# One hybrid layer on one core: larger mixer transfers, a lighter second gate-up group, another order in the second down run

## The chip, the core and the metric

The kernel computes one encoder layer on one NeuronCore of a Trainium2 chip. TensorE (PE; its weight loads are PEld) multiplies matrices, VectorE (DVE) and ScalarE (ACT) do elementwise work, GpSimd (POOL) does a little, and SyncE (SP) issues nearly all transfers from device memory. The metric is the device time of one execution in microseconds. The median of three runs of the kernel before is 1865.89 us (1864.14 to 1866.34).

## The reference, cut to what matters

```
x: (1, 256, 2048) float32, all weights float32; D_FF = 5632
x = x + 0.5 * post1(swiglu_1(pre1(x)))            # gate_up 2048 x 11264, down 5632 x 2048
h = pre_m(x);  p = h @ w_mix_in                   # 2048 x 6656
   p -> q, i, f_fwd, f_bwd, g (1024 columns each) | attention q (1024), k, v (256 each)
y_h = bidirectional gated linear recurrence per head, normalised, times silu(g)
y_a = attention within +-128 positions, with a sink logit and a relative bias
x = x + post_m(concat(y_h, y_a) @ w_mix_out)      # 2048 x 2048
x = x + 0.5 * post2(swiglu_2(pre2(x)))
```

With 256 rows of x, every weight is used once per execution and has to come from device memory.

## The kernel before, in words

**Products.** To keep float32 accuracy each operand is split into a high part h and a low part l, and each product is made of three matmuls: h with h, l with h, h with l. The split of a weight tile of 128x1024 is a cast on ACT (L186) followed by a subtraction on DVE (L187). A weight block arrives as 1 MB in a tile `raw` (three of them, and a part of the tile `rooms` as a fourth while the FFN runs), in two transfers of 512 KB issued by SP (L162), and is split in two halves into tiles h and l, of which there are five each.

**Plain and seven.** FFN and output projections work on blocks u of 256 rows of the weight by 1024 columns, for two row blocks m and two column blocks n. A plain block takes eight products (24 matmuls of 512 columns, `plain`). A seven (`seven`, L455 on) forms sums of the weight's quarters on DVE (L466, L470, L472) and of the activations, and needs seven products (21 matmuls); four of the seven go to PSUM banks of their own and are folded into the results at the end of the run (`fold`, L509 to L517). Its last split half can only be cast when L472 is done. `self.sums` holds the blocks for which sums of activations exist. A down or output run that follows a seven with a plain block loads the plain block and splits its first half inside the seven (`AHEAD`).

**One FFN.** The gate and up projections run in 11 column groups of 512 (`Gated`, eight blocks u each, L938 on in `ffn`). In group 0 the activations are not yet scaled by the row statistics, and no sums exist. While it runs, `even(u)` multiplies each block's activations by a power of two (L877) and, for blocks 1, 3 and 5 (`MIXED_IN`), forms their sums (L883, L390 to L394, then a split). All eight calls of `even` are made during blocks 4 to 7 of group 0. Groups 1 to 10 have three sevens each. After each group `units` applies silu (L900) and the product (L901), transposes (L912) and splits the result into `ht` (L920 and L187). The down projection (`Pairs`) makes two runs over 22 blocks, each run for one half of the 2048 columns, with 11 sevens per run (the even blocks up to 16, and 20 and 21); a list per run in `orders` gives the order. The end of the second run (`finish`) is written out by hand, together with the first products of the stage that follows.

**The mixer.** `w_mix_in` is loaded in 52 blocks of 1 MB, by `source_N` (3-D source, 4 or 8 row tiles) and `chunk_T` (8 row tiles), all through `load` (L149). Products of four head pairs are interleaved with the recurrence and the attention of earlier heads (`side_step`): softmax (L1394), transposes of the probabilities (L1409), their copy to SBUF on ACT (L1412, tile `pt`) and their product with v (L1420). The recurrence needs a logarithm (L1222) and several exponentials (L1240, L1242, L1250, L1257), the gates need a sigmoid (L1327, L1444, L1445); a change of function family on ACT comes with an `ACT_TABLE_LOAD`.

**What sets the order.** Outside the stretches under `manual_schedule` a scheduler of the framework orders each engine's instructions from its own estimates of when operands are ready; on the chip each engine then executes its list in order, and waits on semaphores. So an edit at one place can reorder instructions at others.

Of the kernel before, what the change touches and what calls it, by code (L numbers as in the profile page):

```python
# [24 lines left out]
KT = D // P  # L25
# [12 lines left out]
def hymba_layer_kernel(  # L38
# [41 lines left out]
    def pa():  # L80
        return psum.tile([P, 512], F32, tag="pa", name=nm("pa"))

    def pb():
        return psum.tile([P, 512], F32, tag="pb", name=nm("pb"))
# [59 lines left out]
    def new_raw():  # L144

        raw_places.append(raw_places.pop(0))
        return raw_places[-1]

    def load(src, between=None):  # L149
        raw = new_raw()  # L150
        if len(src.shape) == 4:

            dst = raw.rearrange("p (a n b) -> p a n b", a=src.shape[1], n=src.shape[2])
            parts = [(dst[:, a], src[:, a]) for a in range(src.shape[1])]
        else:
            n = src.shape[1]
            dst = raw.rearrange("p (a b) -> p a b", a=n)
            parts = [(dst[:, a : a + n // 2], src[:, a : a + n // 2]) for a in (0, n // 2)]
        for i, (to, of) in enumerate(parts):
            if i and between:  # L160
                between()
            nc.sync.dma_start(to, of)  # L162
        return raw

    def split_load(src, hp=hip, lp=lop, between=None, middle=None):
        return split(load(src, between), hp, lp, middle)
# [230 lines left out]
    class Blocks:  # L397
# [7 lines left out]
        def __init__(self, tiles, sums):  # L405
            self.tiles, self.sums = tiles, sums

        def begin(self, order, c=None):

            self.order, self.pos, self.seen = order, 0, {}  # L410
            self.c = c or [[pa(), pa()], [pb(), pb()]]
            self.p = None
            at = [i for i, u in enumerate(order) if u in self.sums]
            some = len(at)
            plain = len(order) - some
            self.after = at[-1] + 1 if at else len(order) - 1

            self.rest = 6 * (len(order) - self.after - 1)
            self.of = {}
            for i in range(4):  # L420
                self.of["p", i] = 3 * some
                self.of["c", i // 2, i % 2] = 6 * plain + (3 * some if i < 3 else 0)
# [103 lines left out]
        def work(self, upto):  # L526

            while self.pos < upto:
                u = self.order[self.pos]
                if u in self.sums:  # L530
                    v = self.order[self.pos + 1]
                    if self.AHEAD and v not in self.sums and self.pos + 1 < upto:
                        self.ahead = [v]
                        self.seven(u, self.begin_next)
                    else:
                        self.seven(u)
                else:
                    if self.ahead:
                        _, raw, h, l = self.ahead
                        self.ahead = None  # L540
                        hs, ls = zip((h, l), split_half(raw, 1))
                    else:
                        hs, ls = split_load(self.source(u))
                    if self.pos == self.after + 1:
                        self.fold()
                    places = [(k, m, n) for k in range(2) for m in range(2) for n in range(2)]
                    if self.pos in (self.after, self.after + 1):

                        places.sort(key=lambda at: at[1:])
                    for k, m, n in places:  # L550
                        self.plain(u, hs, ls, m, n, k)
                self.pos += 1
# [251 lines left out]
    MIXED_IN = (1, 3, 5)  # L804
# [5 lines left out]
    class Gated(Blocks):  # L810
# [6 lines left out]

        def group(self, g, c=None):
            self.g = g
            self.begin([0, 2, 1, 4, 3, 5, 6, 7] if g == 1 else range(KT // 2), c)  # L820

        def source(self, u):
            return self.w[:, 2 * u : 2 * u + 2, :, self.g * 512 : (self.g + 1) * 512]
# [30 lines left out]
    def ffn(gated, w_dn, post_gain, again, gain=None, lead=None, aside=None):  # L854

        with ExitStack() as st:
# [78 lines left out]
            for g in range(NG):  # L935
                if g:
                    gated.group(g)
                for u in range(gated.pos, KT // 2):  # L938
                    gated.work(u + 1)
                    if g == 0:  # L940
                        if u == 4:
                            power_and_rest()
                            spread(two)
                        for done in {4: (0, 1, 2), 5: (3, 4), 6: (5, 6), 7: (7,)}.get(u, ()):
                            even(done)
                        if u == 5 and aside:
                            aside()
                        if u == 6:
                            raw_places.append(where_X_was(2))
                    if waiting and u == 0:  # L950
                        next(waiting)
                waiting = units(gated.c, rest if g else rs2)
                next(waiting)
# [1 line left out]
            orders = [  # L955
                [1, 3, 0, 5, 2, 7, 4, 9, 6, 11, 8, 10, 13, 12, 15, 14, 16, 17, 20, 21, 18, 19],

                [1, 0, 2, 3, 4, 5, 6, 14, 7, 8, 9, 10, 16, 11, 12, 13, 20, 21, 15, 17, 18, 19],
            ]
            sums.update((u, None) for u in MIXED if u not in sums)  # L960
            rows = Pairs(w_dn, orders, hts, sums, work, post_gain, stored=True)
# [126 lines left out]
    def again_from(src):  # L1088
# [6 lines left out]

    vbanks = [pa(), pa()]
    xt = ffn(
        gated,
        w_ffn1_down[0],
# [451 lines left out]
```

## Time and profile before

| | |
|---|---|
| median of three runs (range) | 1865.89 us (1864.14 to 1866.34) |
| the profiled execution: time, span | 1864.14 us, 1862.4 us |
| PE busy, share of the span | 1833.9 us, 98% |
| DVE busy | 1646.6 us, 88% |
| ACT busy | 1111.1 us, 60% |
| mean granted TensorE clock | 0.998 |

The profile is of one execution. A wait that the views print is the idle time of an engine ahead of an instruction, with the instruction that ended it. Matmuls overlap, so a row of one matmul is longer than the distance to the next one. In the order, names carry the program's buffer numbers; the profile leaves them out.

### The profile page before, as it was taken

Reading aid. Unit: us, or ns where it says so; the run is one execution under the profiler, and the core shown is the slowest. Engines: PE = TensorE matmul, PEld = TensorE weight load, DVE = VectorE, ACT = ScalarE, POOL = GpSimd, SP = SyncE. Lnnn points to the kernel's source line nnn. Section 1 sums busy time; section 2 is a strip of 40 time slices with the busy share of each in tenths; the row PEclk is TensorE's granted clock in tenths of the full one; section 3 lists DMA queues with packets and bytes.
Section 4 is the critical chain, followed back from the end, with each engine's and each line's share of the span. In section 5 each row is a group of like instructions: output and inputs, shape, how many; then the busy total and the mean of one; then the engine's idle time right before and its main releaser. Section 6 shows DMA issues by size and latency. Waiting matters only on the chain.

```text
span 1862.4 us, 24094 instructions
## 1 busy us (share of the span) xinstructions
PE 1833.9 (98%) x8598; PEld 1518.4 (82%) x8598; DVE 1646.6 (88%) x2080; ACT 1111.1 (60%) x1477; POOL 32.7 (2%) x61
## 2 busy tenths in 40 slices
PE   9999999999999999999999999999999999999998
PEld 7788888888888787888888887778888888888786
DVE  7999999999999997577777887999999999899996
ACT  6555556555655555577677655656556555555563
POOL 1000000000000000000000000000000000000000
PEclk9999999999999999999999999999999999999999
DMA  8566656666877775665564565666666665687774
GB/s 285 167 226 228 204 193 206 221 205 204 288 264 261 259 249 203 194 185 152 161 182 138 181 204 180 219 209 211 222 205 214 221 214 200 228 285 258 246 271 160
DMA packets 192889, 400.45 MB, mean 215 GB/s; under 512 B 12809, under 2 KB 60001, under 8 KB 192001
## 3 DMA queue, kind: packets, MB, share of 16 engines
q1 hardware_dynamic: 189248, 387.25, 63.0%
q0 software_dynamic: 3520, 11.67, 1.6%
q8 instruction: 67, 1.10, 0.2%
q14 instruction: 54, 0.43, 0.1%
HBM read 383.12 MB, written 15.75 MB: 214 GB/s over the span
## 4 chain that ended last, share of the span: by engine, by line
PE 71%; DVE 15%; issue 5%; ACT 4%; DMA 4%; POOL 0%; SPq 0%; DVEq 0%; ACTq 0%; POOLq 0%
PE pa L433 29%; PE pb L433 27%; DVE l L187 7%; PE pa L309 6%; PE pa L314 3%; ACT h L186 2%; DMA raw<-in_w_ffn_down_dram 1%; DMA bias<-row 1%; PE pa L364 1%; PE pa L362 1%; PE pa L363 1%; DVE raw L470 1%; DVE raw L472 1%; DVE raw L466 1%; DMA rooms<-in_w_ffn_down_dram 1%
## 5 line engine op out<-in xcount | busy, mean ns | idle before, releaser
L186 ACT CAST h<-raw 128x1024 fp32r<-128x1024 f32 (+1 forms) x691 | 681.1, 1014 | 455.5 <-DVE raw L472 139.4
L187 DVE TENSOR_TENSOR l<-raw,h 128x1024 fp32r<-128x1024 f32 (+1 forms) x691 | 795.7, 1175 | 96.4 <-ACT h L186 57.7
L433 PE MATMUL pa<-h,xt 128*128 128x512 f32 x1168 | 407.2, 393 | 0.4 <-ACT h L186 0.2
L433 PE MATMUL pb<-h,xt 128*128 128x512 f32 x1048 | 366.0, 391 | 0.0
L433 PEld LDWEIGHTS pa<-h,xt 128*128 128x128 f32 x1168 | 219.5, 188 | 46.5 <-ACT h L186 2.1
L433 PEld LDWEIGHTS pb<-h,xt 128*128 128x128 f32 x1048 | 197.0, 188 | 40.9 <-ACT h L186 0.2
L433 PE MATMUL pa<-l,xt 128*128 128x512 f32 x584 | 227.9, 391 | 0.0
L433 PE MATMUL pb<-l,xt 128*128 128x512 f32 x524 | 204.4, 390 | 0.0
L186 ACT CAST h<-rooms 128x1024 fp32r<-128x1024 f32 (+1 forms) x142 | 145.9, 1044 | 69.6 <-DVE rooms L472 39.2
L187 DVE TENSOR_TENSOR l<-rooms,h 128x1024 fp32r<-128x1024 f32 (+1 forms) x142 | 170.0, 1213 | 14.2 <-ACT h L186 14.0
L309 PE MATMUL pa<-xt,h 128*128 128x512 f32 x672 | 165.4, 395 | 0.0
L433 PE MATMUL pa<-h,ht 128*128 128x512 f32 x440 | 156.5, 392 | 1.5 <-DVE pa L511 1.1
L433 PE MATMUL pb<-h,ht 128*128 128x512 f32 x440 | 155.1, 391 | 0.4 <-DVE pb L515 0.4
L309 PEld LDWEIGHTS pa<-xt,h 128*128 128x128 f32 x672 | 123.5, 189 | 23.5
L433 PEld LDWEIGHTS pa<-l,xt 128*128 128x128 f32 x584 | 110.0, 188 | 22.7 <-DVE l L187 0.5
L433 PEld LDWEIGHTS pb<-l,xt 128*128 128x128 f32 x524 | 98.5, 188 | 20.4
L466 DVE TENSOR_TENSOR raw<-raw 128x1024 f32<-128x1024 f32 x92 | 112.4, 1222 | 0.6
L433 PEld LDWEIGHTS pa<-h,ht 128*128 128x128 f32 x440 | 82.7, 188 | 20.5 <-DVE pa L514 1.8
L433 PEld LDWEIGHTS pb<-h,ht 128*128 128x128 f32 x440 | 82.7, 188 | 18.3 <-DVE pb L515 1.3
L314 PE MATMUL pa<-xt,l 128*128 128x256 f32 x672 | 92.6, 288 | 0.0
L433 PE MATMUL pb<-h,xs 128*128 128x512 f32 x240 | 88.4, 397 | 2.5 <-ACT h L186 2.1
L314 PEld LDWEIGHTS pa<-xt,l 128*128 128x128 f32 x672 | 88.1, 193 | 3.3
(278 smaller groups left out, 2505.9 us busy)
## 6 DMA issues: line engine op xcount, KB each, us to landing
raw<-in_w_ffn_gate_up_dram SPq DMA_DIRECT2D x270, 512.0 KB, 4.9
raw<-in_w_ffn_down_dram SPq DMA_DIRECT2D x132, 512.0 KB, 5.2
raw<-in_w_mix_in_dram SPq DMA_DIRECT2D x104, 512.0 KB, 4.3
rooms<-in_w_ffn_gate_up_dram SPq DMA_DIRECT2D x80, 512.0 KB, 5.3
rooms<-in_w_ffn_down_dram SPq DMA_DIRECT2D x44, 512.0 KB, 5.0
sp<-ss SPq DMA_DIRECT2D x44, 512.0 KB, 6.5
raw<-in_w_mix_out_dram SPq DMA_DIRECT2D x32, 512.0 KB, 4.7
ss<-rooms POOLq DMA_DIRECT2D x22, 512.0 KB, 2.9
```

Source lines behind the costliest of these rows:

```text
L186: nc.scalar.copy(hi, src)
L187: nc.vector.tensor_tensor(lo, src, hi.bitcast(F32), ALU.subtract)
L309: nc.tensor.matmul(slot[f], weights(hs, kk, f), xcol(xt, k), start=(k == 0), stop=(k == KT - 1))
L314: nc.tensor.matmul(slot[f][:, 0:T], weights(ls, kk, f), xcol(xt, kh * 8 + kk, 0), start=False, stop=False,)
L362: nc.tensor.matmul(dst, xh, h[:, o : o + n], start=(k == 0), stop=False)
L363: nc.tensor.matmul(dst, xh, l[:, o : o + n], start=False, stop=False)
L364: nc.tensor.matmul(dst, xl, h[:, o : o + n], start=False, stop=(k == KT - 1))
L433: nc.tensor.matmul(self.bank(at), lhs, rhs, start=(n == 1), stop=n in (ends, self.of[at]), skip_group_check=n > ends,)
L466: nc.vector.tensor_tensor(four[:, 0:2], four[:, 0::3], four[:, 1:2].to_broadcast([P, 2, 512]), ALU.add)
L470: nc.vector.tensor_tensor(b22, b11, b22, ALU.add)
L472: nc.vector.tensor_tensor(b21, b22, b21, ALU.add)
```

## The change

Three edits. First, `load` brings a 3-D source in one transfer unless it has exactly two row tiles; these, the blocks of the down and output projections, still come in two. So the 52 blocks of `w_mix_in` come in one transfer of 1 MB each; gate-up blocks have a 4-D source and are as before. Second, group 1 of each gate-up takes its blocks in natural order and has sevens for blocks 3 and 5 only (`begin` gets a list `some`; block 1 becomes plain), and `even(6)` and `even(7)` are called within group 1, after its blocks 1 and 2. Third, the second down run has another order, in which blocks 2 and 3 change places and blocks 14 and 16 stand later.

```diff
@@ load
             n = src.shape[1]
             dst = raw.rearrange("p (a b) -> p a b", a=n)
-            parts = [(dst[:, a : a + n // 2], src[:, a : a + n // 2]) for a in (0, n // 2)]
+            parts = [(dst, src)]
+            if n == 2:
+                parts = [(dst[:, a], src[:, a]) for a in range(2)]
@@ Blocks.begin
-        def begin(self, order, c=None):
+        def begin(self, order, c=None, some=None):
+            self.some = {u for u in some or order if u in self.sums}
...
-            at = [i for i, u in enumerate(order) if u in self.sums]
+            at = [i for i, u in enumerate(order) if u in self.some]
@@ Blocks.work
-                if u in self.sums:
+                if u in self.some:
                     v = self.order[self.pos + 1]
-                    if self.AHEAD and v not in self.sums and self.pos + 1 < upto:
+                    if self.AHEAD and v not in self.some and self.pos + 1 < upto:
@@ Gated.group
-            self.begin([0, 2, 1, 4, 3, 5, 6, 7] if g == 1 else range(KT // 2), c)
+            self.begin(range(KT // 2), c, MIXED_IN[1:] if g == 1 else MIXED_IN)
@@ ffn
                     gated.work(u + 1)
+                    if g == 1 and 1 <= u <= 2:
+                        even(u + 5)
...
-                        for done in {4: (0, 1, 2), 5: (3, 4), 6: (5, 6), 7: (7,)}.get(u, ()):
+                        for done in {4: (0, 1, 2), 5: (3, 4), 6: (5,)}.get(u, ()):
...
-                [1, 0, 2, 3, 4, 5, 6, 14, 7, 8, 9, 10, 16, 11, 12, 13, 20, 21, 15, 17, 18, 19],
+                [1, 0, 3, 2, 4, 5, 6, 7, 8, 14, 9, 10, 11, 12, 16, 13, 20, 21, 15, 17, 18, 19],
```

The added lines shift the numbers: a line of the old file is called by a number higher by 2 to 5 in the new one.

DVE at the start of group 1 of the first FFN, before: the products of group 0's units (`L901`), the splits `l`, the sums of the first seven's weights (`L466`, `L470`, block 1 in `rooms`), and the results' split `ht`.

```order
L901 SCALAR_TENSOR_TENSOR rooms_473<-pa_120,scales,rooms_473 128x512
L187 TENSOR_TENSOR l_727<-rooms_473,h_726 128x512
L901 SCALAR_TENSOR_TENSOR rooms_473<-pb_122,scales,rooms_473 128x512
L466 TENSOR_TENSOR rooms_473<-rooms_473 128x1024
L187 TENSOR_TENSOR l_732<-rooms_473,h_731 128x1024
L390 TENSOR_TENSOR rooms_473<-rooms_473 128x256
L470 TENSOR_TENSOR rooms_473<-rooms_473 128x512
L187 TENSOR_TENSOR ht_677<-rooms_473,ht_677 128x2x256
L393 TENSOR_TENSOR rooms_473<-rooms_473 128x128
L187 TENSOR_TENSOR ht_687<-pb_667,ht_687 128x2x256
L394 TENSOR_TENSOR rooms_473<-rooms_473 128x128
L187 TENSOR_TENSOR l_737<-rooms_473,h_736 128x1024
```

The same place now: `rooms` holds plain block 2, the first seven is block 3 in `raw_114`, and the scaling of block 7 (`L880`, before `L877`) stands here.

```order
L904 SCALAR_TENSOR_TENSOR rooms_473<-pa_120,scales,rooms_473 128x512
L189 TENSOR_TENSOR l_730<-rooms_473,h_729 128x1024
L904 SCALAR_TENSOR_TENSOR rooms_473<-pb_122,scales,rooms_473 128x512
L880 TENSOR_TENSOR xt_127<-xt_127,R 128x1024
L189 TENSOR_TENSOR l_761<-raw_114,h_760 128x512
L392 TENSOR_TENSOR rooms_473<-rooms_473 128x256
L469 TENSOR_TENSOR raw_114<-raw_114 128x1024
L189 TENSOR_TENSOR ht_675<-rooms_473,ht_675 128x2x256
L395 TENSOR_TENSOR rooms_473<-rooms_473 128x128
L189 TENSOR_TENSOR ht_685<-pb_665,ht_685 128x2x256
L396 TENSOR_TENSOR rooms_473<-rooms_473 128x128
L189 TENSOR_TENSOR l_766<-raw_114,h_765 128x1024
```

The first seven is now the fourth block of the group instead of the third, and one scaling has moved in ahead of its weight sums.

ACT in the mixer before, ahead of the copies `pt` of the first attention heads (`kx`, `qd` and `sg` are the recurrence's exponentials and the gate's sigmoid, `yh` the cast of the gated result):

```order
L1250 ACT_TABLE_LOAD
L1250 ACTIVATE kx_7478<-cum_7468 128x128 x2
L186 CAST h_7379<-raw_114 128x1024
L1327 ACT_TABLE_LOAD
L1327 ACTIVATE sg_7242<-g_7236 128x512
L186 CAST h_7417<-raw_112 128x1024
L1240 ACT_TABLE_LOAD
L1240 ACTIVATE qd_7472<-dm_7470 128x512
L186 CAST yh_7247<-ot_6973 128x2x256
L1412 COPY pt_7290<-pb_7291 128x4x128
L1412 COPY pt_7290<-pb_7297 128x4x128
```

And now:

```order
L1245 ACTIVATE qd_7436<-dm_7434 128x512
L1247 ACTIVATE kd_7438<-dm_7434 128x512
L796 COPY g_7204<-pa_7101 128x256
L796 COPY g_7204<-pa_7102 128x256
L188 CAST h_7340<-raw_114 128x1024
L1255 ACTIVATE kx_7442<-cum_7432 128x128 x2
L188 CAST h_7344<-raw_114 128x1024
L1262 ACTIVATE qx_7443<-cum_7432 128x256
L188 CAST h_7381<-raw_112 128x1024
L1332 ACT_TABLE_LOAD
L1332 ACTIVATE sg_7210<-g_7204 128x512
L1417 COPY pt_7257<-pb_7258 128x4x128
```

The logarithm and its table load (`L1227`, before `L1222`) now stand ahead of the softmax, so that all exponentials follow each other: of three table loads ahead of `pt` in this piece one is left, `yh` has moved behind `pt`, and `kd` and `qx` have moved ahead of it. PE's order in the mixer is the same as before.

DVE in the second down run of the first FFN, before: `la` begins a seven, `L466`, `L470` and `L472` are its weight sums. `raw_114` is block 0, `raw_112` block 2, `raw_113` the plain block 3.

```order
L187 TENSOR_TENSOR la_5052<-raw_112,ha_5051 128x512
L466 TENSOR_TENSOR raw_112<-raw_112 128x1024
L187 TENSOR_TENSOR l_5017<-raw_114,h_5016 128x1024
L187 TENSOR_TENSOR l_5057<-raw_112,h_5056 128x1024
L187 TENSOR_TENSOR l_5062<-raw_112,h_5061 128x1024
L470 TENSOR_TENSOR raw_112<-raw_112 128x512
L187 TENSOR_TENSOR l_5067<-raw_113,h_5066 128x1024
L472 TENSOR_TENSOR raw_112<-raw_112 128x512
```

And now, with `raw_112` the plain block 3, `raw_113` block 2 and `rooms` block 4:

```order
L189 TENSOR_TENSOR la_5076<-raw_113,ha_5075 128x512
L189 TENSOR_TENSOR l_5015<-raw_114,h_5014 128x1024
L189 TENSOR_TENSOR l_5044<-raw_112,h_5043 128x1024
L469 TENSOR_TENSOR raw_113<-raw_113 128x1024
L189 TENSOR_TENSOR l_5081<-raw_113,h_5080 128x1024
L189 TENSOR_TENSOR la_5122<-rooms_473,ha_5121 128x512
L473 TENSOR_TENSOR raw_113<-raw_113 128x512
L189 TENSOR_TENSOR l_5086<-raw_113,h_5085 128x1024
L475 TENSOR_TENSOR raw_113<-raw_113 128x512
```

The second half of the plain block 3 and the first operations of block 4 now stand among those of block 2. On the whole PE has six matmuls more, ACT eight table loads fewer, and SP 52 mixer transfers fewer.

## The prediction, made before the run

> **What bounds the kernel now.** I read the page first (busy time, then the chain of work that ended last), then what PE waits for, then PE by stretches.
>
> ```profile
> span 1862.4 us, 24094 instructions
> PE 1833.9 (98%) x8598; PEld 1518.4 (82%) x8598; DVE 1646.6 (88%) x2080; ACT 1111.1 (60%) x1477; POOL 32.7 (2%) x61
> PE 71%; DVE 15%; issue 5%; ACT 4%; DMA 4%; POOL 0%; SPq 0%; DVEq 0%; ACTq 0%; POOLq 0%
> ...
> PE pb L1420 <- ACT pt L1412: 4.9, 3, 1.9
> PE pb L433 <- ACT h L186: 4.0, 5, 1.1
> ```
>
> PE is the bound, and the chain runs mostly through it. The last two rows, of PE's waits (us in total, times, longest), are where it starves longest: a copy on ACT in the mixer, and the cast of a weight half. Both are touched by the change. So it can win only what PE waits there, and loses each matmul that it adds. The stretches show how much (us, then busy time and instructions of each engine; the last two numbers are the transfer engines' share and GB/s):
>
> ```profile
> 60.00:104.00 44.00, 42.10 (x185) 33.42 (x185) 42.45 (x52) 24.15 (x30) 0.59 (x1) 1.00 0.66 216
> 163.00:206.00 43.00, 43.00 (x195) 35.46 (x194) 40.99 (x48) 25.65 (x30) 0.53 (x1) 1.00 0.62 209
> 1200.00:1244.00 44.00, 42.70 (x188) 33.69 (x187) 42.51 (x54) 26.52 (x32) 0.60 (x1) 1.00 0.61 203
> ...
> 163.25 2.72 PE pa L433 x12
> ```
>
> The second row is a later group without waits: 195 PE instructions in 43.00 us, 0.2205 each. Group 1 of the first FFN lies in the first row: 185 instructions would need 40.8 us and took 44.00, so 3.2 us are lost. For the second FFN: 188 x 0.2205 = 41.45, so 2.55 lost. The last row, of the chain, gives the price of one matmul of 512 columns: 2.72 / 12 = 0.227 us.
>
> **Group 1: two sevens in place of three.** The longest wait of group 1 is that of its first seven for the last cast:
>
> ```profile
> 74.40 0.50 PE L433 MATMUL pb<-h,xs 128*128 128x512 f32 x1 [1.08 <-ACT h L186]
> ...
> 72.59 0.69 DVE L472 TENSOR_TENSOR rooms<-rooms 128x512 f32<-128x512 f32 x1
> 690.85 5.76 DVE L187 TENSOR_TENSOR l<-raw,h 128x1024 fp32r<-128x1024 f32 x5
> ```
>
> ACT is idle ahead of that cast; DVE is late with L472. DVE's prices, start to start: an operation of 1024 columns about 1.14 (last row: 5.76 / 5 with the tail of the fifth), one of 512 about 0.60 (run 2's rows below: 612.17 to 612.77). A seven has four of the first and three of the second: 6.4 us on DVE against 21 x 0.227 = 4.76 on PE. A plain block has two: 2.3 against 24 x 0.227 = 5.44. So a seven costs the lead 1.65 us, a plain block restores 3.1. A group has slack on average, but group 1 starts with DVE behind: `even`, the sums and group 0's results come in the same 25 us.
>
> Now one plain block more stands ahead of the first seven: PE asks 5.44 us later. DVE's added work up to that point, by the order, is two splits of that plain block, 2.3 us; in the second FFN the moved L880 stands ahead too, but it stood ahead of the old first seven as well. The new margin is 5.44 - 2.3 - 1.25 (the wait, with the distance to the next matmul) = about 1.9 us; the second seven has a plain block before it and keeps about 2. So the waits go. `even(6)` and `even(7)` cost 1.14 each as before and are needed only by blocks 6 and 7, over 20 us later; without that cover a late one would cost PE up to 1.14. I take back 5.2 of the 5.75 us (bounds: 3.0, if the interleaved remainder stays, and 5.75). **The price:** block 1 as a plain block has three matmuls more, in two FFNs six: 6 x 0.227 = +1.36 us, all on PE.
>
> **Second down run.** Blocks 0 and 2 are two sevens in a row, right after DVE's work on the first run's results:
>
> ```profile
> 612.17 0.68 DVE L470 TENSOR_TENSOR raw<-raw 128x512 f32<-128x512 f32 x1
> 612.77 1.22 DVE L187 TENSOR_TENSOR l<-raw,h 128x1024 fp32r<-128x1024 f32 x1
> 613.90 0.69 DVE L472 TENSOR_TENSOR raw<-raw 128x512 f32<-128x512 f32 x1
> 614.70 2.00 ACT L186 CAST h<-raw 128x1024 fp32r<-128x1024 f32 x2 [3.24 <-DVE raw L472]
> 615.80 0.50 PE L433 MATMUL pb<-h,sp 128*128 128x512 f32 x1 [0.93 <-ACT h L186]
> ...
> 1753.63 0.50 PE L433 MATMUL pb<-h,sp 128*128 128x512 f32 x1 [0.93 <-ACT h L186]
> 683.43 1.23 DVE L187 TENSOR_TENSOR l<-rooms,h 128x1024 fp32r<-128x1024 f32 x1 [1.19 <-ACT h L186]
> ```
>
> Same place, same size in both FFNs: 0.93 plus 0.16 of spacing, 1.09 us each. With plain block 3 between, block 2 is asked for 5.44 later and DVE's L472 for it ends about 1.7 later (by the order: one split, one `la`, then the same operations), a margin of 2.65. The next pair, 2 and 4, takes 1.65 of it and the early half of block 5 another 1.14: about -0.1 to -0.7 left. So 1.09 becomes 0 to 0.7 per FFN. **What is late next:** later pairs stand at 8-14 and 12-16, and after 12-16 comes one plain block and then 20-21. The lead is capped by the five tiles (last row: DVE itself stands idle there, waiting for a cast). With a cap near 3.5 us the two pairs end at about 0: 3.5 - 1.65 - 1.65 = 0.2, +3.1, -3.3 = 0.0. I take 0 there, between +1.5 per FFN (one cast and some) and -1.0 (the fold after block 21 comes earlier). Together -0.8 per FFN, **-1.6** (bounds -4.2 and +2).
>
> **Mixer.** The transfers are the edit, but what reaches PE is the new order on ACT:
>
> ```profile
> 871.70 1.28 ACT L1240 ACT_TABLE_LOAD   x1
> 872.99 0.63 ACT L1240 ACTIVATE qd<-dm 128x512 f32<-128x512 f32 x1
> 873.53 0.60 ACT L186 CAST yh<-ot 128x512 fp32r<-128x512 f32 x1
> 874.04 1.06 ACT L1412 COPY pt<-pb 128x512 f32<-128x512 f32 x2
> ...
> 868.55 1.04 PE L1409 MATMUL pb<-ident,sc 128*128 128x128 f32 x8
> 874.67 1.59 PE L1420 MATMUL pb<-pt,va 128*128 128x256 f32 x6 [1.85 <-ACT pt L1412]
> 943.26 1.99 PE L1420 MATMUL pb<-pt,va 128*128 128x256 f32 x8 [1.80 <-ACT pt L1412]
> 1009.74 2.00 PE L1420 MATMUL pb<-pt,va 128*128 128x256 f32 x8 [1.25 <-ACT pt L1412]
> 862.67 1.14 DVE L1401 TENSOR_SCALAR sc<-sc,sm 128x256 f32<-128x256 f32 x4
> ```
>
> The transposes (L1409) are done near 869.6; `pt` waits behind ACT's own work until 874.04. Ahead of it two table loads go (2 x 1.29 with the step to the next row) and `yh` (0.51); `kd` (0.53) and `qx` (about 0.4) come: -2.1 us, more than the 1.85. The logarithm ahead of the softmax delays L1401 by 1.28 + 0.54 = 1.8; it ended at 863.8 and PE asks at 868.55, so 4.7 us cover it. In the third pair two loads go as well, but two casts (1.0 each) move ahead of `pt`: -0.5 of 1.25. Sum: 1.85 + 1.80 + 0.5 = 4.15; I take **-4.0** (bounds -5.5, all three with their spacing, and 0).
>
> On these switches the Trainium skill ("ScalarE: Activation LUTs", What ACT_TABLE_LOAD costs) says that each costs about 2.66 us, 1283 ns of load and a drain of similar length. The load agrees with 1.28; no drain follows it here, since the next operation starts at 872.99. With the page's figure the third wait would go too, and the sum below be about 0.8 lower.
>
> The transfers themselves: a first half can be cast only when all of its 1 MB has landed.
>
> ```profile
> L162 SPq DMA_DIRECT2D raw<-in_w_mix_in_dram x104: 367/368/384, 693.2 to 1025.9; - x104
>   ACT h L186: 0.3, 1
> DMA to landing us min/median/max: 3.3/4.3/9.3
> ...
> ACT h L186 <- PE pa L309: 25.6, 26, 3.2
> ...
> 1030.77 1.04 ACT L186 CAST h<-raw 128x1024 fp32r<-128x1024 f32 x1 [0.79 <-PE pa L309]
> ```
>
> Only one cast ever waited for mixer weights (0.3 us, at the very start); the others wait for PE to free a tile. No row shows a lone 1 MB transfer. Lower bound 4.3 (the median of a half), upper 9.3 (the slowest half, queued behind others); nearest is two halves issued together, so I take about 5. The tightest place is the last block: issued at 1025.9, cast at 1030.77, 4.9 us: barely hidden, and behind it PE has four more tiles in hand. So 0. SP also issues the reload of x at the end of the FFN behind two mixer transfers now; that is hidden by blocks 15, 17 and half of 18 and 19 (72 matmuls, 16.3 us of PE) that stand ahead of its first use, and would cost what is over if a landing took longer. SP's 52 saved issues are on no path.
>
> **Sum** against the profiled execution (1864.14 us, span 1862.4): +1.36 - 5.2 - 1.6 - 4.0 = -9.4, so 1854.7. That execution is the fastest of the three; their median lies 1.75 above it. I predict **1855.5 us**.
>
> **Rivals.** (a) The order on ACT doesn't reach PE: the exponentials now wait for `dm`, or a cast ahead of `pt` waits for its weights. For it: ACT's list is in order and had hardly a gap there. Against: 2 us to spare. -9.4 + 4.0 = about 1859.5. (b) The relocated pairs stall: run 2 gains nothing and costs 1.5 per FFN at 20-21, -9.4 + 1.6 + 3 = about 1860. (c) The change doesn't do what it says: groups 1 and run 2 exchange one wait for another and +1.36 remains beside a small mixer gain: 1863 to 1867, no change. (d) Slower: mixer weights become late. Its point is a landing time above 4.9 us at the tail; at 9.3 us the cast at 1030.77 would be 4.4 late, and the blocks near it alike. The other blocks have more room, 5 to 15 us by the same comparison of issue and cast. With an estimated 2.1 us for each of some eleven blocks, 23 us of cast waits, half of them passed to PE, and the 5.4 us of groups and run 2 kept: about 1870. For it: three `raw` tiles only, and both halves must now be free. Against: 172 GB/s in the mixer and hardly a DMA wait. The Trainium skill ("Perfetto Trace Analysis", DMA Optimizations) says that splitting transfers may let some work start sooner where the transfer engines are idle; by that rule (d) is what merging them would bring. Here casts wait for tiles, not for weights.
>
> **How the numbers follow.** Forecast 0.55; (a) 0.14; (b) 0.13; (c) 0.12; (d) 0.06. About 0.2% (3.7 us) is what a measurement here can tell from no change. Faster: forecast, (a) and (b), 0.82; same: (c), 0.12; slower: (d), 0.06. The forecast's own bounds reach 1850 (all waits gone) and 1860; taking in (a) and (b), the range is 1850 to 1862.
>
> **What would show it.** Groups: no wait of L433 for L186 between 60 and 104 us, and near 0.2205 us per PE instruction there. Run 2: no 0.93 us wait at the second seven; any wait at 20-21 is (b). Mixer: L1420 waits under 1 us in total, eight table loads fewer on ACT, and no `in_w_mix_in` among ACT's releasers; if that appears, (d). I am wrong if PE's waits move instead of going.

## The result, and the profile after

The changed kernel takes **1851.32 us** (median of four runs, 1850.18 to 1852.26) against 1866.12 us of the kernel before (1864.14 to 1868.33): a ratio of 0.992, 95% interval 0.9903 to 0.9937. It is 14.8 us faster, where 9.4 us were forecast. The profiled execution has a span of 1848.6 us, 13.8 less than the profiled one before.

The page of the changed kernel (span, busy times, shares of the chain), and below the dots what PE waits for (us in total, times, longest):

```profile
span 1848.6 us, 23953 instructions
PE 1827.9 (99%) x8604; PEld 1516.6 (82%) x8604; DVE 1638.0 (89%) x2070; ACT 1099.6 (59%) x1465; POOL 32.5 (2%) x61
PE 77%; DVE 12%; issue 4%; DMA 3%; ACT 3%; POOL 0%; DVEq 0%; ACTq 0%; SPq 0%; POOLq 0%
...
PE pb L436 <- DVE l L189: 3.1, 6, 1.1
PE pb L280 <- DVE dg L279: 1.7, 2, 0.9
```

Both rows that led the list before are gone: the copy `pt` in the mixer (4.9 us) and the cast in front of `pb` (4.0 us). In their place a split half `l` leads with 3.1 us.

Group 1 by stretches; the second row starts 8 us earlier than its counterpart before, because what stands above it, the mixer most of all, is shorter:

```profile
60.00:104.00 44.00, 44.00 (x200) 36.41 (x199) 42.30 (x52) 25.84 (x32) 0.59 (x1) 1.00 0.66 215
1192.00:1236.00 44.00, 44.00 (x204) 36.35 (x203) 41.75 (x51) 26.28 (x32) 0.60 (x1) 1.00 0.57 190
```

PE fits 200 and 204 instructions into the 44 us that held 185 and 188, and never stands idle. (Of the 204, 16 are transposes of about 0.11 us each; the other three stretches hold eight.)

The mixer, PE's product with v (L1425) in the order of time, and the transposes (L1414) ahead of the third:

```profile
870.34 1.99 PE L1425 MATMUL pb<-pt,va 128*128 128x256 f32 x8
935.66 1.99 PE L1425 MATMUL pb<-pt,va 128*128 128x256 f32 x8
996.63 1.03 PE L1414 MATMUL pb<-ident,sc 128*128 128x128 f32 x8
1000.73 1.89 PE L1425 MATMUL pb<-pt,va 128*128 128x256 f32 x8
```

None of the three carries a bracket with a wait; before they waited 1.85, 1.80 and 1.25 us.

The second down run, the longest wait of each FFN:

```profile
625.11 0.50 PE L436 MATMUL pb<-l,sp 128*128 128x512 f32 x1 [1.11 <-DVE l L189]
...
1750.71 0.50 PE L436 MATMUL pb<-l,sp 128*128 128x512 f32 x1 [1.10 <-DVE l L189]
```

Here a wait has moved rather than gone. The 0.93 us at the second seven (block 2) are no longer there; one seven later, at block 4, which is now the second of the pair 2-4, PE waits 1.1 us.

**Where the 13.8 us lie.** For a table over whole stages I counted the time lost on PE: for each matmul the distance from its start to the start of the next, less the median distance of matmuls of that line and width (0.227 us for 512 columns), summed between the same points of the program, both FFNs together. A loss that lies in the program as a regular pattern counts as well, so the sum never gets to zero. The mixer is counted here from its first product with `w_mix_in`. The expectations of the runs below count it from the end of the down projection; that adds 3.5 us in each trace.

| us lost on PE in one trace | group 1 | first down runs | second down runs | mixer | all the rest | sum |
|---|---|---|---|---|---|---|
| before | 6.6 | 2.8 | 6.0 | 9.6 | 13.8 | 38.7 |
| changed | 0.5 | 1.6 | 5.0 | 2.6 | 14.3 | 23.9 |
| changed, another execution | 0.5 | 3.0 | 5.3 | 2.7 | 14.2 | 25.7 |
| only one transfer | 6.6 | 0.6 | 4.5 | 2.4 | 14.4 | 28.4 |
| only group 1 | 0.5 | 1.1 | 4.9 | 9.9 | 14.7 | 30.9 |
| only the second run's order | 6.6 | 1.4 | 4.7 | 6.4 | 13.6 | 32.7 |
| before, `pt` copied by DVE | 6.6 | 1.9 | 5.4 | 4.0 | 15.0 | 33.0 |
| changed, 8 mixer blocks in halves | 0.5 | 4.6 | 4.4 | 2.7 | 13.6 | 25.8 |
| changed, evens in group 0 | 0.5 | 4.7 | 5.3 | 2.6 | 13.1 | 26.2 |
| changed, three sevens | 7.2 | 1.9 | 5.2 | 2.9 | 14.1 | 31.2 |
| changed, pair 4-6 | 0.7 | 1.2 | 7.5 | 2.1 | 13.9 | 25.4 |
| changed, ten sevens | 0.5 | 1.6 | 3.3 | 2.6 | 14.7 | 22.7 |
| all blocks in one transfer | 0.5 | -0.3 | 5.3 | 1.2 | 12.0 | 18.7 |
| the same with ten sevens | 0.5 | -0.3 | 1.4 | 1.4 | 12.0 | 15.0 |

From the first row to the second: -6.1 in group 1, -6.9 in the mixer, -1.0 in the second down runs, -1.3 in the first ones, +0.5 elsewhere, and six matmuls more (8604 against 8598) at 0.227 us, +1.4. That makes -13.4, close to the span's -13.8. The lower rows are the experiments. Two single traces stand behind this account; the section on the prediction says how far other comparisons agree.

### The profile page after: what moved, and what is told of

It is laid out like the page before. It is cut to its first block, busy times and chain, and to the rows that moved or that the text cites. A ratio compares the mean times of both kernels' runs of the same rounds, so it can differ in the third digit from the quotient of the medians.

```text
span 1848.6 us, 23953 instructions
## 1 busy us (share of the span) xinstructions
PE 1827.9 (99%) x8604; PEld 1516.6 (82%) x8604; DVE 1638.0 (89%) x2070; ACT 1099.6 (59%) x1465; POOL 32.5 (2%) x61
## 4 chain that ended last, share of the span: by engine, by line
PE 77%; DVE 12%; issue 4%; DMA 3%; ACT 3%; POOL 0%; DVEq 0%; ACTq 0%; SPq 0%; POOLq 0%
PE pa L436 31%; PE pb L436 28%; PE pa L311 8%; DVE l L189 7%; PE pa L316 4%; ACT h L188 2%; PE pa L366 1%; PE pa L364 1%; PE pa L365 1%; DMA raw<-in_w_ffn_gate_up_dram 1%; DVE raw L475 1%; DMA raw<-in_w_ffn_down_dram 1%; DVE raw L473 1%; DVE raw L469 1%; ACT xt L239 1%
## 5 line engine op out<-in xcount | busy, mean ns | idle before, releaser
L188 ACT CAST h<-rooms 128x1024 fp32r<-128x1024 f32 x138 | 142.5, 1051 | 70.1 <-DVE rooms L475 42.0
L189 DVE TENSOR_TENSOR l<-rooms,h 128x1024 fp32r<-128x1024 f32 x138 | 165.9, 1219 | 14.3 <-ACT h L188 14.0
L436 PE MATMUL pa<-l,ht 128*128 128x512 f32 x220 | 85.7, 390 | 0.0
```

Source lines behind the costliest of these rows:

```text
L188: nc.scalar.copy(hi, src)
L189: nc.vector.tensor_tensor(lo, src, hi.bitcast(F32), ALU.subtract)
L436: nc.tensor.matmul(self.bank(at), lhs, rhs, start=(n == 1), stop=n in (ends, self.of[at]), skip_group_check=n > ends,)
```

## Experiments

Each ran beside the kernel before on one chip. There the kernel before had medians of 1861.2 to 1863.7 us, so ratios are what to compare.

### One edit at a time

**Only the one-transfer edit**, on the kernel before:

```diff
-            parts = [(dst[:, a : a + n // 2], src[:, a : a + n // 2]) for a in (0, n // 2)]
+            parts = [(dst, src)]
+            if n == 2:
+                parts = [(dst[:, a], src[:, a]) for a in range(2)]
```

> The kernel before with only the first edit: blocks of w_mix_in come in one transfer each. Theory 1 (the order on ACT is what counts): ACT has 30 table loads as in the changed kernel, the three waits of L1420 (4.9 us in total before) are gone or under 0.5 us together, and the time falls by the mixer's part of the trace difference, 6 to 7 us, so a ratio of 0.9962 to 0.9970. The prediction's own term was 4.0 us (0.9979). Rival: the mixer waits went for another reason (the other edits shift when DVE and ACT enter the mixer), then the L1420 waits stay above 2 us and the ratio is above 0.998. Rival (d), late weights: ACT's casts wait for in_w_mix_in transfers by more than 5 us in total and the time does not fall.

Measured: 1855.56 us, ratio 0.9959 (0.9943 to 0.9975). ACT has 30 table loads, no product with v waits over 0.5 us, and the mixer loses 2.4 us instead of 9.6. No cast waits for `w_mix_in` in this trace. So the edit brings its gain without the other two, and more of it than the 4.0 us forecast.

**Only the group-1 edit** (`some`, natural order, `even(6)` and `even(7)` in the group), on the kernel before:

```diff
-            self.begin([0, 2, 1, 4, 3, 5, 6, 7] if g == 1 else range(KT // 2), c)
+            self.begin(range(KT // 2), c, MIXED_IN[1:] if g == 1 else MIXED_IN)
...
-                        for done in {4: (0, 1, 2), 5: (3, 4), 6: (5, 6), 7: (7,)}.get(u, ()):
+                        for done in {4: (0, 1, 2), 5: (3, 4), 6: (5,)}.get(u, ()):
```

> The kernel before with only the second edit: two sevens in group 1, and even(6) and even(7) called within it. Theory: PE's waits for the cast and for ht between 60 and 104 us and between 1200 and 1244 us go, 6.0 to 6.7 us of lost PE time less 1.36 us for six matmuls: 4.6 to 5.3 us, a ratio of 0.9971 to 0.9976. The prediction's own terms give 5.2 - 1.36 = 3.8 us (0.9979). Rival: part of the gain is passed on and lost in later groups or in the down run, then under 3 us (above 0.9984).

Measured: 1857.32 us, ratio 0.9972 (0.9955 to 0.9988). Group 1 loses 0.5 us instead of 6.6, and nothing comes back in the later groups. The mixer, whose lists are as before, waits as before (PE's waits of this kernel):

```profile
PE pb L1423 <- ACT pt L1415: 5.5, 3, 2.6
```

**Only the second run's order**, on the kernel before:

```diff
-                [1, 0, 2, 3, 4, 5, 6, 14, 7, 8, 9, 10, 16, 11, 12, 13, 20, 21, 15, 17, 18, 19],
+                [1, 0, 3, 2, 4, 5, 6, 7, 8, 14, 9, 10, 11, 12, 16, 13, 20, 21, 15, 17, 18, 19],
```

> The kernel before with only the third edit, the order of the second down run. Theory of the prediction: 0.8 us less per FFN, 1.6 us in all, a ratio of 0.9991, with no wait above 0.7 us in the two runs' second halves. Theory from the changed kernel's trace: the 0.93 us wait moves from the pair 0-2 to the pair 2-4 (1.1 us about 9 us later) and only the fold's waits fall, 0 to 0.5 us per FFN: a ratio of 0.9994 to 1.0000, not told from no change. Rival (b): 1.5 us lost per FFN at 20-21, a ratio of 1.0016 or less.

Measured: 1861.15 us, ratio 0.9989 (0.9977 to 1.0), not told from no change. The wait moves to the pair 2-4 here too (the longest of the second row). Its mixer shows something else: with ACT's list as before there, the third wait is missing in this execution. Of PE's waits two rows (total, times, longest):

```profile
PE pb L1420 <- ACT pt L1412: 3.7, 2, 2.2
PE pb L433 <- DVE l L187: 2.6, 3, 1.1
```

So the third of the three waits hangs on how PE and ACT happen to stand to each other: it was 1.25 us in the trace of before and nothing in this one. The old mixer's loss is therefore 6.4 to 9.9 us in three traces, the new one's 2.1 to 2.9 in eight.

### What in the one-transfer edit does it: the transfers or ACT's list?

**Some of the 52 mixer blocks back in halves**, on the changed kernel. Only blocks with eight row tiles stay in one transfer. ACT's list is then the same, instruction for instruction.

```diff
-            parts = [(dst, src)]
-            if n == 2:
-                parts = [(dst[:, a], src[:, a]) for a in range(2)]
+            parts = [(dst[:, a : a + n // 2], src[:, a : a + n // 2]) for a in (0, n // 2)]
+            if n == 8:
+                parts = [(dst, src)]
```

> The changed kernel, but of the 52 mixer blocks only the 40 with eight row tiles come in one transfer; the 12 with four row tiles come in two halves as before. ACT's order is instruction for instruction that of the changed kernel. If ACT's order is what counts, the time is that of the changed kernel: 1851.3 us, a ratio of 0.992, L1420 waits none. If the number and size of the transfers counts, 12 of the 52 blocks are back in halves and about a quarter of the mixer's 6 to 7 us is lost again: 1.6 us, a ratio of 0.9929.

Measured: 1851.23 us, ratio 0.9932 (0.9914 to 0.995); the mixer loses 2.7 us, as in the changed kernel. The expectation counts 12 blocks in halves, but the page of this run has 44 of the 52 still whole, so they are eight:

```profile
raw<-in_w_mix_in_dram SPq DMA_DIRECT2D x44, 1024.0 KB, 5.0
```

With 8 of the 52 blocks back in halves nothing changes in the mixer. That is a weak test of the size of the transfers, since 44 blocks keep theirs.

**`pt` copied by DVE**, on the kernel before: half transfers, 38 table loads, ACT's list as it was but without the copies and with a few neighbours (`kd`, one cast) in other places.

```diff
-                nc.scalar.copy(
+                nc.vector.tensor_copy(
                     pt[:, j].rearrange("p s (m c) -> p (s m) c", c=P)[:, :, ::-1],
```

> The kernel before, with its half transfers, but the copies pt of the attention's probabilities are made by DVE instead of ACT; the rest of ACT's list is as before, with its 38 table loads. Theory (pt waits behind ACT's list; the one-transfer edit helped only by that list's new order): the three waits of L1420 go without any larger transfer, the mixer loses 6 to 8 us in place of 10 to 13.4, a ratio of 0.9965 to 0.9975. Rival (the larger transfers themselves, or the fewer table loads, free PE at other places): then the copies on DVE remove the L1420 waits but less than 3 us, a ratio above 0.9984. Third: DVE's list is no shorter at that place, the copies wait there too, and L1420 waits 1 to 2 us as before.

Measured: 1858.06 us, ratio 0.9972 (0.9959 to 0.9984). PE's waits in front of the product with v:

```profile
PE pb L1420 <- DVE pt L1412: 1.0, 3, 0.5
PE pb L1420 <- ACT g L793: 0.3, 1, 0.3
```

The 4.9 us fall to 1.3, and the mixer's loss to 4.0, without any larger transfer and without one table load less. So `pt` was late because of what stood ahead of it in ACT's list. The rest, from 4.0 to some 2.6 us, came only with the new list and the larger transfers together; these two runs do not divide it.

### Group 1: two sevens or moved evens?

**Three sevens in the old order, with the evens moved**, on the changed kernel:

```diff
-            self.begin(range(KT // 2), c, MIXED_IN[1:] if g == 1 else MIXED_IN)
+            self.begin([0, 2, 1, 4, 3, 5, 6, 7] if g == 1 else range(KT // 2), c)
```

> The changed kernel, but group 1 has three sevens in the old order 0, 2, 1, 4, 3, 5, 6, 7, with even(6) and even(7) still moved into the group. It tells what two sevens are worth apart from the moved evens. Prediction's theory (the plain block ahead makes the margin): without it the 1.1 us wait for the cast at the first seven returns, reduced by at most the 2.3 us of two evens: lost PE time in group 1 between 1.5 and 3.9 us per FFN, against 0.4 in the changed kernel and 3.9 and 3.4 before. Rival (the moved evens alone gave DVE the time): 0.4 us lost per FFN, and six matmuls fewer on PE make it 1.36 us faster than the changed kernel.

Measured: 1858.7 us, ratio 0.9972 (0.996 to 0.9984): group 1's gain is gone. It loses 2.8 us in the first FFN and 4.4 in the second, against 3.5 and 3.1 before. PE in group 1 of the first FFN:

```profile
74.31 0.73 PE L436 MATMUL pa<-h,xt 128*128 128x512 f32 x2 [0.21 <-ACT h L188]
88.19 0.50 PE L436 MATMUL pa<-h,xs 128*128 128x512 f32 x1 [0.26 <-ACT h L188]
89.63 0.50 PE L436 MATMUL pb<-h,xs 128*128 128x512 f32 x1 [0.71 <-ACT h L188]
```

The 1.08 us wait of the first seven has gone with the two evens that no longer stand ahead of it, but they now stand between the sevens, and the wait at 89.63 doubles from 0.34 to 0.71. Its counterpart before:

```profile
90.14 0.50 PE L433 MATMUL pb<-h,xs 128*128 128x512 f32 x1 [0.34 <-ACT h L186]
```

In the second FFN the loss is larger than before the change, and above the 3.9 us that the theory allowed.

**Two sevens, with the evens in group 0**, on the changed kernel:

```diff
-                    if g == 1 and 1 <= u <= 2:
-                        even(u + 5)
...
-                        for done in {4: (0, 1, 2), 5: (3, 4), 6: (5,)}.get(u, ()):
+                        for done in {4: (0, 1, 2), 5: (3, 4), 6: (5, 6), 7: (7,)}.get(u, ()):
```

> The changed kernel, but even(6) and even(7) stand in group 0 again. The other half of the same question. Prediction's theory: the plain block gives 1.9 us of margin with the evens left where they were, so lost PE time in group 1 stays at 0.4 to 0.6 us per FFN and the time is that of the changed kernel. Rival: the evens are what counts, and 1.5 to 3 us per FFN come back, +3 to +6 us.

Measured: 1851.51 us, ratio 0.9935 (0.9909 to 0.996); group 1 loses 0.5 us. The plain block does all of it. Moving the evens is worth nothing beside it, and without it the group lost 0.6 us more in the one trace taken. A plain block both puts the first seven later and takes work from DVE; no run parts these two.

### The second down run

**The first pair one plain block later**, on the changed kernel:

```diff
-                [1, 0, 3, 2, 4, 5, 6, 7, 8, 14, 9, 10, 11, 12, 16, 13, 20, 21, 15, 17, 18, 19],
+                [1, 0, 3, 2, 5, 4, 6, 7, 8, 9, 10, 14, 11, 12, 16, 13, 20, 21, 15, 17, 18, 19],
```

> The changed kernel with the first pair of sevens in the second down run one plain block later: 1, 0, 3, 2, 5, 4, 6, 7, 8, 9, 10, 14, 11, 12, 16, 13, 20, 21, 15, 17, 18, 19. Theory (the lead of DVE over PE grows by each plain block that stands between sevens, and at 2-4 it had not grown enough): the wait of 1.1 us (1.27 with its spacing) at the second seven of 2-4 goes in both FFNs, and lost PE time in the two second runs falls from about 4.8 to 2.5 us. Rival: the lead is no larger after block 5, since a seven and a plain block nearly cancel, and the wait stands at the pair 4-6 with the same size: 4.8 us lost as before. Either way the median moves by at most 2.5 us, a ratio of 0.991 to 0.993 to the kernel before; the verdict is read from the waits.

Measured: 1851.65 us, ratio 0.9937 (0.9918 to 0.9956). The second run of the first FFN, PE's waits of 0.5 us and more:

```profile
633.05 0.50 PE L436 MATMUL pb<-l,sp 128*128 128x512 f32 x1 [0.51 <-DVE l L189]
...
674.83 0.50 PE L436 MATMUL pb<-l,sp 128*128 128x512 f32 x1 [0.98 <-DVE l L189]
```

The first is at the pair 4-6, the second at 12-16. The lead does grow with a plain block (1.11 falls to 0.51), but PE waits again further on, and the two runs lose 7.5 us instead of 5.0. So neither forecast of the loss held (2.5 and 4.8 us): this order moved the wait and made the sum larger.

**Ten sevens instead of eleven** (block 4 plain), on the changed kernel, with its order:

```diff
-            self.begin(self.orders[now])
+            order = self.orders[now]
+            self.begin(order, None, [u for u in order if u != 4] if self.stored and now else None)
```

> The changed kernel with ten sevens instead of eleven in the second down run: block 4 is plain there, the order as it is. The same trade as in group 1: three matmuls more per FFN, 1.36 us in all, and no pair at 2-4. Theory: the 1.1 us wait at 2-4 goes in both FFNs and no other takes its place, since DVE has 6.4 - 2.3 = 4.1 us less to do; lost PE time in the two second runs falls from about 4.9 to 2 us, so 1 to 1.5 us faster than the changed kernel, which the median can hardly tell (ratio 0.991 to 0.993). Rival: the wait moves on to 8-14 and 12-16, as it moved when the pair did; then 4.5 us stay lost and the kernel is 1 us slower than the changed one.

Measured: 1851.08 us, ratio 0.9954 (0.9938 to 0.997). The wait at 2-4 goes, and smaller ones remain. The second runs lose 3.3 us against 5.0 and 5.3, and six matmuls cost 1.4: a gain of at most half a microsecond, which no median here can show.

**The changed kernel again**, for a second trace:

> The changed kernel again, for a second trace and a time on this chip beside the other two. If what differs from trace to trace in the first down runs (0.0 to 2.9 us lost per FFN in eight traces, whose order there is one and the same) is not the kernel's doing, this trace has another value there than the first (1.78 and 0.09 us), while the mixer stays at 5.6 to 6.4 us lost, group 1 at 0.3 to 0.6 us per FFN and the second down runs at 4.5 to 5.4 us together. Ratio to the kernel before 0.992 to 0.994.

Measured: 1850.77 us, ratio 0.9947 (0.993 to 0.9963). The first down runs lose 3.0 us here against 1.6, the other stages what they lost. In the twelve traces with half transfers for the down projection the lists of all engines in the first down runs are the same, and these runs lost between 0.6 and 4.7 us. The time on this chip is 10.4 us below the kernel before (1861.21), where the first comparison gave 14.8.

### One transfer where casts wait for weights

**All blocks in one transfer**, on the changed kernel:

```diff
             parts = [(dst, src)]
-            if n == 2:
-                parts = [(dst[:, a], src[:, a]) for a in range(2)]
```

> The changed kernel, but the blocks of the down and output projections come in one transfer of 1 MB too. In those stages casts do wait for transfers (in the changed kernel ACT's ha waits 15.3 us for in_w_ffn_down, 9 times), while in the mixer only one cast does. Theory (a larger transfer costs where casts wait for weights, and only there): the waits of ACT for in_w_ffn_down rise to 25 us or more, lost PE time in the four down runs from about 7 to 10 us to 11 to 18 us, and the kernel is 3 to 8 us slower than the changed one, a ratio of 0.994 to 0.997 to the kernel before. Rival (one transfer is as good as two halves anywhere, or better): the lost time of the runs stays at 7 to 10 us, a ratio of 0.992 to 0.9935.

Measured: 1845.6 us (1845.17 to 1845.77), ratio 0.992 (0.9906 to 0.9935), 5.2 us below the changed kernel on the same chip. My theory fell: the four down runs lose 5.0 us together, less than the rival's 7 to 10. Transfers of the down projection, in the changed kernel (who waits for them, then the landing times):

```profile
L164 SPq DMA_DIRECT2D raw<-in_w_ffn_down_dram x132: 327/328/424, 461.1 to 1816.2; - x132
...
  ACT ha L188: 18.7, 12
  DVE rooms L469: 2.9, 2
  ACT h L188: 0.7, 2
...
DMA to landing us min/median/max: 3.5/5.1/7.4
```

and with all blocks in one transfer:

```profile
L162 SPq DMA_DIRECT2D raw<-in_w_ffn_down_dram x66: 367/368/397, 462.0 to 1809.9; - x66
...
  ACT ha L186: 22.1, 16
...
DMA to landing us min/median/max: 4.8/5.5/8.7
```

1 MB lands in 5.5 us, 0.4 us later than 512 KB. The wait of the first cast of a seven rises only from 18.7 to 22.1 us, and the waits of DVE and of later casts for a second half vanish. In sum these waits hardly change (22.3 to 22.1 us), so they alone don't say why PE loses less. Pairing the issues in the trace of the changed kernel, the second half of a block is issued 1.74 us after the first (median), and the block is complete 7.1 us after its first issue; in one transfer it is complete after 5.5. A seven reads both halves in its first weight sum, so for it the whole block counts. That this is the cause is argued from these rows; the larger transfers also change the order on ACT and DVE in the down runs, and no run divides the two. What is shown: the first down runs lose nothing any more (0.6 to 4.7 us with halves), in this and in the next kernel. They are only a part of the 5.2 us. The output projection, whose 16 blocks come whole now too, loses nothing either (1.9 us in the changed kernel, 1.2 to 2.4 with halves; it stands under "all the rest"), and the mixer, whose last products are in another order, 1.4 us less.

The Trainium skill ("Perfetto Trace Analysis", DMA Optimizations) says that splitting transfers may let some work start sooner where transfer engines are idle. A first half does land sooner here, by about 0.7 us (4.8 against 5.5 us, medians), but the whole kernel was not done sooner. The rule's condition was hardly met: over the first down run of the changed kernel the engines were busy for a share of 0.80.

**The same with ten sevens in the second run**, two plain blocks ahead of the first seven:

```diff
-            self.begin(self.orders[now])
+            order = self.orders[now]
+            self.begin(order, None, [u for u in order if u != 4] if self.stored and now else None)
...
-                [1, 0, 3, 2, 4, 5, 6, 7, 8, 14, 9, 10, 11, 12, 16, 13, 20, 21, 15, 17, 18, 19],
+                [1, 3, 0, 4, 2, 5, 6, 7, 8, 14, 9, 10, 11, 12, 16, 13, 20, 21, 15, 17, 18, 19],
```

> The kernel with all blocks in one transfer, and ten sevens in the second down run in the order 1, 3, 0, 4, 2, 5, 6, 7, 8, 14, 9, 10, 11, 12, 16, 13, 20, 21, 15, 17, 18, 19 (block 4 plain, two plain blocks ahead of the first seven, which is where that kernel lost 2.0 us in the first FFN and 0.7 in the second). Theory: those waits go, lost PE time in the two second runs falls from 5.4 to about 2 us, less 1.36 us for six matmuls: 2 us faster than the kernel with all blocks in one transfer, a ratio of 0.990 to 0.9915 to the kernel before. Rival: the waits move on to the pairs 8-14 and 12-16 as they did when the pair was moved, 5 us stay lost and it is 1.4 us slower, a ratio of 0.992 to 0.9935.

Measured: **1843.19 us** (1842.32 to 1843.73), ratio 0.9896 (0.9879 to 0.9912), the fastest version. The second down runs lose 1.4 us instead of 5.3; less 1.4 for the matmuls that is 2.5 us gained, and the medians of the two kernels, taken in two comparisons, differ by 2.4. The run changes the order and the number of sevens together, so it does not say which of them did it.

## Why the prediction was right, and where its steps were off

| term | predicted | in the two traces | what other traces say |
|---|---|---|---|
| six matmuls | +1.4 | +1.4 | |
| group 1 | -5.2 | -6.1 | 6.6 with the old group, 0.5 to 0.7 with the new one |
| second down runs | -1.6 | -1.0 | old order 4.5 to 6.0, new order 4.4 to 5.3: -0.2 between the means |
| mixer | -4.0 | -6.9 | old 6.4 to 9.9, new 2.1 to 2.9: -6.0 between the means |
| first down runs, lists unchanged | 0 | -1.3 | 0.6 to 4.7 in the twelve traces with half transfers |
| all the rest | 0 | +0.5 | 13.1 to 15.0 in the same traces |

The range held the time, the likeliest value was 4 us too slow, and the case that happened is the forecast's own: groups and mixer give the gain. Of the rivals none came true as a whole. By its own sum (1854.7 for the profiled execution, and 1.75 more for the median) the likeliest value would have been 1856.5; the prediction takes 1855.5 and gives no reason.

How large the gain is, is less certain than the two traces make it look. On the chip of its second trace the changed kernel was 10.4 us faster, a ratio of 0.9947 (0.993 to 0.9963), close to the 9.4 us of the sum. The 13.8 us between the two traces hold 1.3 us of chance in the first down runs, and a trace of the kernel before in whose mixer three waits stood, where another trace with the same list on ACT had two.

**Group 1: right mechanism, term mis-sized.** The plain block ahead of the first seven makes the margin, and the evens cost nothing, as said; the runs with the one and without the other show both. I took back 5.2 of 5.75 us and kept the rest for an interleaved remainder. There was none: all of the loss went, 6.1 us as the table counts it, and by that count the upper bound was a little too low.

**Second down run: the step that failed is "1.09 becomes 0 to 0.7".** The margin for block 2 was right, its wait went. But I gave the pair 2-4 a lead of -0.1 to -0.7, and it lost 1.27 in the first FFN and 1.26 in the second. Nothing stalled at 20-21; there is 0.39 lost at 8-14 in the second FFN. That is rival (b)'s mechanism at another place and at about the old price, so the edit as a whole gave nothing that can be measured. I followed the lead to the first pair and not through the whole run: moving the pair again moved the wait again (7.5 us lost), and taking one seven away lowered the loss to 3.3 us. It is not that DVE lacks time for eleven sevens as a whole. With all blocks in one transfer DVE is busy for 105.30 of 114 us in the second run of the first FFN,

```profile
602.00:716.00 114.00, 112.14 (x492) 90.80 (x491) 105.30 (x121) 65.86 (x82) 1.12 (x3) 1.00 0.67 249
```

and for 106.67 in the first run (its row stands in the last section), which has eleven sevens in another order and loses nothing. What is left as a cause is the order, and how far behind DVE enters the run; that is argued, not shown. Which order would serve the second run best stays open, since no run gave it that of the first.

**Mixer: right mechanism, the third wait miscounted.** That `pt` waits behind ACT's own list was borne out by the copies on DVE. That transfers matter only through this list's order was borne out in the main: without any larger transfer 5.6 of some 7 us went, and the rest is not divided. Of the three waits I let the third fall by 0.5 us only. ACT before, from the first exponential of the softmax to `pt`, with the four table loads between:

```profile
995.59 0.51 ACT L1394 ACTIVATE sc<-sc,mx 128x256 f32<-128x256 f32 x1 [1.38 <-DVE mx L1377]
...
999.08 1.28 ACT L1222 ACT_TABLE_LOAD   x1 [0.37 <-DVE sm L1398]
...
1002.50 1.28 ACT L1250 ACT_TABLE_LOAD   x1
...
1005.56 1.28 ACT L1445 ACT_TABLE_LOAD   x1
...
1007.50 1.28 ACT L1257 ACT_TABLE_LOAD   x1
...
1009.12 1.05 ACT L1412 COPY pt<-pb 128x512 f32<-128x512 f32 x2
```

And ACT after, the same stretch:

```profile
989.16 0.51 ACT L1399 ACTIVATE sc<-sc,mx 128x256 f32<-128x256 f32 x1
...
996.66 1.28 ACT L1450 ACT_TABLE_LOAD   x1
997.96 0.63 ACT L1450 ACTIVATE zb<-zb 128x512 f32<-128x512 f32 x1
...
999.43 1.07 ACT L1417 COPY pt<-pb 128x512 f32<-128x512 f32 x2
```

From 13.53 to 10.27 us. Three loads have left, not two, and with the logarithm its own 0.5 us and the 0.37 us for which it waited; the two casts that came take 2 us of that back. Against 1.25 us of wait that is ample. The rest of what was missed in the mixer (5.4 us with spacing for the three waits, of 6.9) lies around them, 0.3 us at L1414 among it.

On the table loads, the next operation starts at 997.96, 1.30 us after the load at 996.66: here too, no drain follows. The third wait did go, but because three loads left, at 1.29 us each.

**Rival (d) and the landing time.** 1 MB of `w_mix_in` was estimated to land in about 5 us:

```profile
L164 SPq DMA_DIRECT2D raw<-in_w_mix_in_dram x52: 367/368/384, 692.1 to 1014.4; - x52
...
  ACT h L188: 3.4, 1
...
DMA to landing us min/median/max: 4.9/5.0/8.4
```

That was right. One cast waits 3.4 us, against my sign that none would: it is the first one, at 699.04, while PE is still busy with the down projection, and the loss around it is what it was. So the sign was drawn too tightly; a cast that waits says little while PE has other work.

**First down runs.** The 1.3 us that they gave between the two traces are no effect of the change, since every engine's list there is the same and the loss varies more than that from one execution to the next. The forecast knew nothing of this term.

## What to carry to other kernels

A change to a load can win through the order that it makes the scheduler choose; compare the lists first, and test the list and the load apart. Where heavy blocks follow each other, follow the lead through the whole run: here each new place for a pair only moved the wait, and a lighter block together with a larger margin at the start took most of it away. Before a large transfer is cut into halves, ask when its user needs the whole of it.

## What the runs showed of the hardware that was not expected

1 MB in one transfer lands almost as soon as 512 KB does: 5.0 us against 4.3 for mixer weights, 5.5 against 5.1 for the down projection. Over the first down run of the first FFN the transfer engines were busy for a smaller share while moving as much (the last two numbers of a row are that share and GB/s), first in the changed kernel:

```profile
488.00:602.00 114.00, 113.47 (x501) 92.62 (x500) 106.19 (x120) 64.93 (x78) 1.06 (x2) 1.00 0.80 278
```

and with all blocks in one transfer:

```profile
488.00:602.00 114.00, 114.00 (x509) 94.48 (x508) 106.67 (x121) 67.38 (x79) 1.07 (x2) 1.00 0.74 276
```

The other traces with half transfers have 0.80 to 0.82 there, the second one with whole blocks 0.75. In the mixer, at 172 to 174 GB/s, the share hardly moved: 0.57 with halves, 0.56 with whole transfers (740 to 1060 us, before and after).

A rule of the Trainium skill ("DMA: Bandwidth & Descriptors", Rules for kernel authors) asks for at least 1 MiB per transfer where bandwidth is wanted. The two rows do not show more bandwidth (278 and 276 GB/s), but about the same for a smaller share, 0.74 against 0.80.

And the same list of instructions does not lose the same time in each execution: in the first down runs, where casts wait for transfers, it was 0.6 to 4.7 us with half transfers. With whole ones, and another order on ACT and DVE, it was nothing in two traces.
